# A bidirectional hybrid encoder layer: in its scan one VectorE addition becomes an accumulating DMA, and two VectorE copies move to ScalarE

## The chip, the cores and the metric

The kernel runs on one core of a Trainium2 chip. The metric is device time in microseconds (us) for one execution. A core has TensorE (PE, matrix products; its weight loads are shown as PEld), VectorE (DVE), ScalarE (ACT), GpSimd (POOL) and SyncE (SP), each with an instruction queue of its own that runs in order and waits on semaphores, and 16 engines for DMA transfers, which SP and POOL issue here. SBUF is the on-chip memory with 128 partitions, PSUM the memory that TensorE writes to.

## The reference

One encoder layer over 1024 positions of width 1024: a normalised input is projected to many columns; a convolution branch and a bidirectional gated linear recurrence ("the scan") run side by side; their gated sum is projected and added to the input; a gated feed-forward block with a short convolution follows, and a last norm. The change lies in the scan. Its forward direction is, per head (8 heads of 128 columns):

```python
def _chunk_gated_scan(q, k, v, lf):
    # S_t = diag(f_t) S_{t-1} + k_t v_t^T,  o_t = S_t^T q_t,  lf = log f
    ...
    def step(state, inp):
        qb, kb, vb, lfb = inp
        a = jnp.cumsum(lfb, axis=2)
        diff = a[:, :, :, None, :] - a[:, :, None, :, :]
        decay = jnp.where(tril, jnp.exp(jnp.minimum(diff, 0.0)), 0.0)
        scores = jnp.einsum("bhtk,bhsk,bhtsk->bhts", qb, kb, decay)
        o = (jnp.einsum("bhts,bhsv->bhtv", scores, vb)
             + jnp.einsum("bhtk,bhkv->bhtv", qb * jnp.exp(a), state))
        ...
```

The backward direction is the same on flipped inputs with its own gates, and the two outputs are added: `return o_fwd + o_bwd`. A position therefore meets itself twice, once in each direction. All of it is float32.

## The kernel before

**Stages.** Input norm and the first projections; a convolution of 31 taps on VectorE beside most of the input projections; then, from 540 us to some 990 us, the scan, beside the projections that are left (the generator `dense`); then the output projections, the feed-forward block and the last norm. A float32 product is made of three products of rounded parts (`mm3`, L143 to L145), whose parts ScalarE (L121) and VectorE (L118) prepare.

**Order of the work.** Only TensorE's order is the order in which the program is written (`manual_schedule(engines={PE})`); for the other engines a scheduler plans the order when the program is built, from modelled durations and dependencies, and sets the semaphores.

**The scan.** A head's 1024 positions are taken in two halves of 512, so there are 16 halves, i = 0 to 15, two per head; "even" and "odd" below are by i. In a half, positions lie along the columns, in four chunks of 128. For each half:

- `scan_inputs` (L741) loads q and the gates' inputs and makes the gates `f` and keys `k` with ScalarE (L752, L753, L755) and one VectorE clamp (L762). It is called one half further ahead.
- `scan_base` (L765) works on blocks of eight positions. In the tile DE, made once and used by all halves, it builds running products of gates for both directions: E in its first half, D in its second, eight columns per block, so that the r-th of each block is reached with a stride of eight. L780 copies two such columns, L781 to L798 fill the others with products and a reciprocal (L786). From these it makes Qh (L730 by way of L809) and Kh (L733), then qF and kG. All but the gates is VectorE's. It runs one half ahead, two steps at a time.
- `scan_levels` (L825) makes the 128 x 128 score blocks S_t of the four chunks. Positions that share a block of eight come from `inside(d)`, one product per direction, laid into S_t under the masks m_f and m_b. The backward product's diagonal can't be laid over the forward one, so it is collected under the mask m_d in the tile dg (L867), of which only the diagonal is ever not zero. Then come the levels 8, 16, 32 and 64: at level h each pair of neighbouring blocks of h positions is joined, by a copy A of kG's halves (ScalarE, L835), four matmuls into a PSUM bank (L838), an update of kG, the move of the level's part of the product into S_t, an update of qF (both updates are L730), and a product of the small tile tb. The next level's matmuls need the updated qF. The part that belongs to a level is that in which row and column differ by an exclusive-or from h to 2h - 1: levels 16 and 32 are laid in by VectorE under the masks m_16 and m_32 (L869, all 128 x 512 elements read), level 64 by ScalarE as two blocks of 64 partitions (L873), level 8 is a whole copy by ScalarE (L862) that comes first. Last, L885 adds dg to S_t on VectorE.
- `scan_states` (L887) turns kG over (transposes L894, copies kT L896), forms the chunk's contribution to the states (L903) and carries the states on (L911, L921).
- `outputs` (L985) of a head are made in the steps of the next head's even half: the backward states (L989), then for each half the products with S_t, v and the states (L942), a copy (L944), four Squares with sums (L948), the reciprocal root on POOL (`rstd_small`, L404 and L405), the scaling (L955), a transpose (L963) and VectorE's product `ev` (L965).

**What lies between.** After each step of `scan_levels` and `scan_states`, `between` lets the dense projections advance, then the next half's base, then the outputs of the head before:

```python
            def between(fill):
                dense.fill(fill)
                if ahead is not None:
                    ahead.step(BASE_STEPS)
                pending.fill(1)
```

S_t has three buffers, dg and DE one, qF three. POOL has no DMA to issue during the scan; in the projections before and in the feed-forward block after it, `pair_job` issues accumulating DMAs there (L238).

Of the kernel before, what the change touches and what calls it, by code (L numbers as in the profile page):

```python
# [13 lines left out]
U8 = mybir.dt.uint8  # L14
AF = mybir.ActivationFunctionType
ALU = mybir.AluOpType
AX = mybir.AxisListType

P = 128
# [15 lines left out]
def view(t, off, dims):  # L35

    return bass.AP(
        tensor=t.tensor,
        offset=t.offset + off,
        ap=[list(t.ap[0])] + [list(d) for d in dims],  # L40
    )
# [3 lines left out]
def tile_hybrid_encoder(  # L45
# [24 lines left out]
    V, A, G, T = nc.vector, nc.scalar, nc.gpsimd, nc.tensor  # L70

    S, D = x.shape[1], x.shape[2]
# [10 lines left out]
    cp = ctx.enter_context(tc.tile_pool(name="const", bufs=1))  # L83
# [7 lines left out]
    def nm(s):  # L91
        uid[0] += 1
        return f"{s}_{uid[0]}"
# [3 lines left out]
    def bank(tag):  # L97
        return ps.tile([P, H], F32, tag=tag, name=nm(tag), bufs=BANKS[tag])
# [13 lines left out]
    def load(src):  # L112
        t = tmp()
        nc.sync.dma_start(t, src)
        return t
# [438 lines left out]
    m_b = cp.tile([P, P], U8, name="m_b")  # L554
    m_d = cp.tile([P, P], U8, name="m_d")
    m_16 = cp.tile([P, P], U8, name="m_16")
    m_32 = cp.tile([P, P], U8, name="m_32")

    def build_masks():
        it = mp.tile([P, P], I32, tag="tm", name=nm("it"), bufs=4)  # L560
        ip = mp.tile([P, P], I32, tag="tm", name=nm("ip"), bufs=4)
        G.iota(it, pattern=[[1, P]], base=0, channel_multiplier=0)
        G.iota(ip, pattern=[[0, P]], base=0, channel_multiplier=1)
        xo = mp.tile([P, P], I32, tag="tm", name=nm("xo"), bufs=4)
        V.tensor_tensor(xo, it, ip, op=ALU.bitwise_xor)
        fs = mp.tile([P, 4, P], F32, tag="tm", name=nm("fs"), bufs=4)
        V.tensor_copy(fs[:, 0, :], xo)
        V.tensor_tensor(fs[:, 1, :], it, ip, op=ALU.subtract)
        ge = fs[:, 1, :]
        V.tensor_scalar(m_d, fs[:, 0, :], 0.0, None, op0=ALU.is_equal)  # L570
        V.tensor_scalar(fs[:, 2, :], fs[:, 0, :], 8.0, None, op0=ALU.is_lt)
        V.tensor_scalar(fs[:, 3, :], ge, 0.0, None, op0=ALU.is_ge)
        V.tensor_tensor(m_f, fs[:, 2, :], fs[:, 3, :], op=ALU.mult)
        V.tensor_scalar(fs[:, 3, :], ge, 0.0, None, op0=ALU.is_lt)
        V.tensor_tensor(m_b, fs[:, 2, :], fs[:, 3, :], op=ALU.mult)
        for m, h in ((m_16, 16.0), (m_32, 32.0)):
            V.tensor_scalar(fs[:, 2, :], fs[:, 0, :], h, None, op0=ALU.is_ge)
            V.tensor_scalar(fs[:, 3, :], fs[:, 0, :], 2 * h, None, op0=ALU.is_lt)
            V.tensor_tensor(m, fs[:, 2, :], fs[:, 3, :], op=ALU.mult)

    build_masks()

# [129 lines left out]
    for k in range(NK2):  # L712
        t = load(d_h[k][1])
# [7 lines left out]
    dg = hp.tile([P, H], F32, name="dg")  # L721
# [7 lines left out]
    def tt(o, a, b, op=ALU.mult):  # L729
        V.tensor_tensor(o, a, b, op=op)  # L730

    def keys(o, a, scale, b):
        V.scalar_tensor_tensor(o, a, scale, b, op0=ALU.mult, op1=ALU.mult)  # L733
# [4 lines left out]
    def c4(t):  # L738
        return t.rearrange("p (c t) -> p c t", c=4)
# [25 lines left out]
    def scan_base(ins):  # L765


        q, f, kk, ks = ins

        def two(t, *r):  # L770
            if len(r) == 1:
                return view(t, r[0], [[8, N2]])
            return view(t, r[0], [[r[1] - r[0], 2], [8, N2]])

        fv = lambda *r: two(f, *r)
        ed = lambda *r: two(DE, *r)
        D = D0


        V.tensor_copy(ed(2, D + 4), fv(3, 4))  # L780
        tt(ed(1, D + 5), fv(2, 4), fv(3, 5))  # L781
        yield
        tt(ed(0, D + 6), fv(1, 6), ed(1, D + 5))
        tt(ed(D + 7), ed(D + 6), fv(7))
        yield
        V.reciprocal(ed(D, 7), ed(0, D + 7))  # L786
        yield

        fm = hp.tile([P, 2, NB], F32, tag="fm", name=nm("fm"), bufs=2)
        turned = view(fm, NB, [[-NB, 2], [1, NB]])  # L790
        tt(turned, view(f, 0, [[H, 2], [8, NB]]), view(DE, E0, [[H, 2], [8, NB]]))
        tb = hp.tile([P, 3, NB], F32, tag="tb", name=nm("tb"), bufs=3)
        tt(tb[:, 0:2, :], turned, view(DE, D + 7, [[H, 2], [8, NB]]))
        V.tensor_copy(tb[:, 2, :], tb[:, 0, :])
        tt(ed(D + 1, 6), ed(D, 7), fv(1, 7))
        yield
        tt(ed(D + 2, 5), ed(D + 1, 6), fv(2, 6))
        tt(ed(4), ed(5), fv(5))  # L798
        yield

        qF = hp.tile([P, 2, H], F32, tag="qF", name=nm("qF"), bufs=3)
        kG = hp.tile([P, 2, H], F32, tag="kG", name=nm("kG"), bufs=2)
        Qh = hp.tile([P, 2, H], F32, tag="Qh", name=nm("Qh"), bufs=1)
        Kh = hp.tile([P, 2, H], F32, tag="Kh", name=nm("Kh"), bufs=1)
        along = [[8, NB], [1, 8]]
        for d in range(2):
            m0, st = ((0, 1), (7, -1))[d]
            whole = [[8, NB], [st, 8]]
            tt(view(Qh, (1 - d) * H + m0, whole), view(q, m0, whole), view(DE, D + d * H, along))  # L809
            yield  # L810
            keys(
                view(Kh, d * H + m0, whole),
                view(kk, d * H + m0, whole),
                ks[:, d : d + 1],
                view(DE, d * H, along),
            )
            yield
        both = [[H, 2], [8, NB], [1, 8]]
        tt(view(qF, 0, both), view(Qh, 0, both), view(fm, 0, [[NB, 2], [1, NB], [0, 8]]))
        yield  # L820
        tt(view(kG, 0, both), view(Kh, 0, both), view(DE, D + 7, [[H, 2], [8, NB], [0, 8]]))
        yield
        yield qF, kG, [(Qh[:, 1 - d, :], Kh[:, d, :]) for d in range(2)], tb

    def scan_levels(base, S_t, Tt):  # L825


        qF, kG, qk, tb = base

        def pairs(t, h):  # L830
            return view(t, 0, [[2 * h, H // (2 * h)], [H + h, 2], [1, h]])

        def level(h):
            A_t = page(hp, "A", 2)
            A.copy(A_t.rearrange("p (b x e) -> p b x e", x=2, e=h), pairs(kG, h))  # L835
            b = bank("sc")
            for c in range(4):
                T.matmul(  # L838
                    b[:, c * P : (c + 1) * P].rearrange("p (b x e) -> p b x e", x=2, e=h),
                    A_t[:, c * P : (c + 1) * P],  # L840
                    view(qF, c * P, [[2 * h, P // (2 * h)], [H + h, 2], [1, h]]),
                    start=True,
                    stop=True,
                )
            return c4(b)

        def inside(d):
            b = bank("ob" if d else "sc")
            for c in range(4):
                sl = slice(c * P, (c + 1) * P)  # L850
                T.matmul(b[:, sl], qk[d][1][:, sl], qk[d][0][:, sl], start=True, stop=True)
            return c4(b)

        def over(m):
            return view(m, 0, [[0, 4], [1, P]])

        for h in (8, 16, 32, 64):
            n, nb = H // (2 * h), H // h
            b = level(h)
            tt(pairs(kG, h), pairs(kG, h), view(tb, 1, [[2, n], [nb - 1, 2], [0, h]]))  # L860
            if h == 8:
                A.copy(S_t, b)  # L862
                for d, m in ((0, m_f), (1, m_b)):
                    bi = inside(d)
                    V.copy_predicated(S_t, over(m), bi)
                    if d == 1:
                        V.copy_predicated(c4(dg), over(m_d), bi)  # L867
            elif h < 64:
                V.copy_predicated(S_t, over(m_16 if h == 16 else m_32), b)  # L869
            else:  # L870
                for s0 in range(0, P, h):
                    t0 = s0 ^ h
                    A.copy(S_t[s0 : s0 + h, :, t0 : t0 + h], b[s0 : s0 + h, :, t0 : t0 + h])  # L873
            tt(pairs(qF, h), pairs(qF, h), view(tb, nb + 1, [[2, n], [nb - 1, 2], [0, h]]))
            if h < 64:
                tn = hp.tile([P, 3, NB], F32, tag="tb", name=nm("tb"), bufs=3)
                k = 3
                to = view(tn, 0, [[n, 3], [1, n]])
            else:
                k = 2  # L880
                to = view(Tt, 0, [[4, 2], [1, n]])
            tt(to, view(tb, 0, [[nb, k], [2, n]]), view(tb, 1, [[nb, k], [2, n]]))
            tb = tn
            yield
        V.tensor_tensor(S_t, S_t, c4(dg), op=ALU.add)  # L885

    def scan_states(i, kG, v, Tt, Sf, Sb):  # L887

# [122 lines left out]
    for h in range(NH):  # L1011
# [4 lines left out]
        for half in range(2):  # L1016
# [11 lines left out]
            S_t = hp.tile([P, 4, P], F32, tag="S", name=nm("S"), bufs=3)  # L1028
            vl = load(d_v[h][half])
            for n, _ in enumerate(scan_levels(base, S_t, Tt[:, half])):  # L1030
                if n == 2:
                    b = bank("tr")
# [339 lines left out]
```

## Time and profile before

The median of three runs is 1899.92 us (1898.41 to 1903.82). One execution was profiled:

| profiled execution | us | share of the span |
|---|---|---|
| its time | 1905.6 | |
| span, first to last instruction | 1903.8 | |
| TensorE busy | 1799.7 | 95% |
| VectorE busy | 1270.2 | 67% |
| ScalarE busy | 799.2 | 42% |
| GpSimd busy | 210.9 | 11% |
| granted TensorE clock, mean | 0.977 | |

The views used below: the page's line of busy times; the table of stretches, whose rows give the stretch, its length and then the busy time and the count of instructions of TensorE, its weight loads, VectorE, ScalarE and GpSimd, then the granted clock, the share of the DMA engines and GB/s; the waits, whose rows name who waited, for whom, the total in us, how often and the longest; the timeline, every instruction with start and duration; and the chain of waits, which is followed back from the last instruction to whatever released each step. Names such as `sc<-qF,A` are output and inputs, buffer numbers left out; where a helper records an operation, the line is the helper's (L730 for every `tt`).

### The profile page before, as it was taken

The page shows a single profiled execution, that of the slowest core. Times are in us where ns is not written, and L with a number is a line of the kernel's source. Part 1 is how long each engine was busy: PE and PEld are TensorE (multiplying, and loading weights), DVE is VectorE, ACT ScalarE, POOL GpSimd, SP SyncE. Part 2 cuts the span into 40 slices and gives each one's busy share as a digit, 9 for nine tenths or more (in the row PEclk, how much of TensorE's full clock was granted, in tenths as well). Part 3 has the DMA queues.
Part 4 walks back from the last instruction along what each step waited for, and adds up shares of the span by engine and source line. Part 5 has one row for each costly group of instructions (what it writes and reads, how often), then busy time and mean ns, then how long its engine had stood idle before and what let it go on. Part 6 is the DMA issues. An engine that isn't in the chain of part 4 may idle for free.

```text
span 1903.8 us, 23750 instructions
## 1 busy us (share of the span) xinstructions
PE 1799.7 (95%) x8543; PEld 1484.0 (78%) x8543; DVE 1270.2 (67%) x1860; ACT 799.2 (42%) x1488; POOL 210.9 (11%) x218
## 2 busy tenths in 40 slices
PE   6988999999999998999998999899999999999996
PEld 5767878887778887888786888588888888788885
DVE  3488999535469898999835555667676666534445
ACT  6433333234554554555443134544343344522124
POOL 3101111213100001000100000111111111000000
PEclk9999999999999999999998999899999999999998
DMA  7747788786563333342237665777676676733134
GB/s 256 219 119 169 179 188 199 185 182 148 190 192 89 113 108 96 111 122 82 75 95 216 197 200 183 185 153 154 147 151 143 143 156 128 221 93 96 54 89 162
DMA packets 323916, 285.09 MB, mean 150 GB/s; under 512 B 14926, under 2 KB 245078, under 8 KB 323798
## 3 DMA queue, kind: packets, MB, share of 16 engines
q1 hardware_dynamic: 272006, 242.67, 41.5%
q0 software_dynamic: 51792, 40.90, 15.2%
q8 instruction: 67, 1.10, 0.3%
q14 instruction: 51, 0.42, 0.1%
HBM read 191.24 MB, written 71.83 MB: 138 GB/s over the span
## 4 chain that ended last, share of the span: by engine, by line
PE 66%; DVE 13%; DMA 8%; ACT 6%; issue 3%; POOL 2%; SPq 0%; ACTq 0%; POOLq 0%; DVEq 0%
PE mm L143 16%; PE mm L144 16%; PE mm L145 16%; PE sc L144 3%; PE sc L145 3%; PE sc L143 3%; PE tr L143 2%; PE tr L144 2%; PE tr L145 2%; DVE wp L118 1%; DVE kG L730 1%; DVE DE L730 1%; PE sc L838 1%; DVE qF L730 1%; DMA wr<-wr 1%
## 5 line engine op out<-in xcount | busy, mean ns | idle before, releaser
L143 PE MATMUL mm<-hx,wp 128*128 128x512 f32 x1176 | 482.6, 410 | 24.6 <-ACT hx L121 8.6
L145 PE MATMUL mm<-hx,wp 128*128 128x512 f32 x1176 | 467.4, 397 | 3.9 <-DVE wp L118 3.9
L144 PE MATMUL mm<-hx,wp 128*128 128x512 f32 x1176 | 466.8, 397 | 2.9 <-POOL hx L118 1.9
L121 ACT CAST wp<-wr 128x1024 fp32r<-128x1024 f32 (+2 forms) x196 | 179.7, 917 | 323.0 <-PE mm L144 222.9
L143 PEld LDWEIGHTS mm<-hx,wp 128*128 128x128 f32 x1176 | 226.5, 193 | 73.7 <-ACT hx L121 9.5
L118 DVE TENSOR_TENSOR wp<-wr,wp 128x1024 fp32r<-128x1024 f32 (+2 forms) x196 | 206.9, 1056 | 102.9 <-ACT wp L121 97.4
L145 PEld LDWEIGHTS mm<-hx,wp 128*128 128x128 f32 x1176 | 225.5, 192 | 55.1 <-DVE wp L118 5.4
L144 PEld LDWEIGHTS mm<-hx,wp 128*128 128x128 f32 x1176 | 226.5, 193 | 48.4 <-POOL hx L118 3.6
L645 DVE SCALAR_TENSOR_TENSOR acc<-gl,v_b,acc 128x1024 f32<-128x1024 f32 x120 | 150.1, 1285 | 0.5
L143 PE MATMUL sc<-hy,wq 128*128 128x512 f32 x244 | 97.3, 399 | 3.1 <-ACT hy L121 3.0
L144 PE MATMUL sc<-hy,wq 128*128 128x512 f32 x244 | 96.7, 396 | 2.7 <-DVE hy L118 2.7
L145 PE MATMUL sc<-hy,wq 128*128 128x512 f32 x244 | 96.2, 394 | 0.0
L238 POOL DMA_DIRECT2D wr<-sw x39 | 34.9, 896 | 519.3 <-DVE wp L118 297.4
L1251 DVE TENSOR_TENSOR xr<-mm,xr 128x512 f32<-128x512 f32 x48 | 33.1, 690 | 82.0 <-PE mm L145 82.0
L838 PEld LDWEIGHTS sc<-qF,A 128*128 128x128 f32 x512 | 65.9, 193 | 19.0 <-issue 13.3
L838 PE MATMUL sc<-qF,A 128*128 128x128 f32 x512 | 69.1, 278 | 11.7 <-DVE qF L730 10.6
L121 ACT CAST wq<-sw 128x1024 fp32r<-128x1024 f32 x39 | 41.1, 1054 | 86.6 <-PE mm L144 66.4
L143 PE MATMUL mm<-hy,wp 128*128 128x512 f32 x156 | 63.2, 405 | 7.4 <-ACT wp L121 5.3
L266 ACT COPY su<-mm 128x512 f32<-128x512 f32 x78 | 45.5, 583 | 53.4 <-PE mm L145 53.4
L835 ACT COPY A<-kG 128x512 f32<-128x512 f32 x64 | 39.7, 620 | 66.3 <-DVE kG L730 37.8
L1169 DVE SCALAR_TENSOR_TENSOR tm<-gp,v_a,tm 128x512 f32<-128x512 f32 x88 | 65.6, 746 | 1.8 <-ACT tm L1165 0.9
L1153 DVE TENSOR_TENSOR ft<-su,mm 128x512 f32<-128x512 f32 x22 | 15.1, 687 | 71.6 <-issue 68.1
(281 smaller groups left out, 3548.6 us busy)
## 6 DMA issues: line engine op xcount, KB each, us to landing
wr<-in_w_in_dram SPq DMA_DIRECT2D x55, 512.0 KB, 6.5
sw<-in_ffn_w_up_dram SPq DMA_DIRECT2D x44, 256.0 KB, 3.5
sw<-in_ffn_w_up_dram POOLq DMA_DIRECT2D x22, 512.0 KB, 8.3
wr<-in_ffn_w_up_dram SPq DMA_DIRECT2D x22, 512.0 KB
d_g<-ft SPq DMA_DIRECT2D x44, 256.0 KB, 5.9
ev<-d_g SPq DMA_DIRECT2D x44, 256.0 KB, 3.2
wr<-sw POOLq DMA_DIRECT2D x39, 256.0 KB, 3.3
wr<-wr POOLq DMA_DIRECT2D x39, 256.0 KB, 3.8
```

The source lines that it names most:

```text
L118: eng.tensor_tensor(lo, src, hi.bitcast(F32), op=ALU.subtract)
L121: A.copy(hi, src)
L143: T.matmul(acc, whi[:, k, :], ahi, start=first, stop=False, skip_group_check=again)
L144: T.matmul(acc, whi[:, k, :], alo, start=False, stop=False, skip_group_check=again)
L145: T.matmul(acc, wlo[:, k, :], ahi, start=False, stop=last, skip_group_check=again)
L238: G.dma_start(o, a, accum_op=ALU.add)
L266: A.copy(t, acc)
L645: V.scalar_tensor_tensor(acc, g[:, k : k + S], tap(k), acc, op0=ALU.mult, op1=ALU.add)
L730: V.tensor_tensor(o, a, b, op=op)
L835: A.copy(A_t.rearrange("p (b x e) -> p b x e", x=2, e=h), pairs(kG, h))
L838: T.matmul(b[:, c * P : (c + 1) * P].rearrange("p (b x e) -> p b x e", x=2, e=h), A_t[:, c * P : (c + 1) * P], view(qF, c * P, [[2 * h, P ...
L1169: V.scalar_tensor_tensor(c, g[:, o + k : o + k + H], vec("fdw", k * NF + j), c, op0=ALU.mult, op1=ALU.add,)
```

## The change

Three edits in the scan, and one tile less:

- The strided copy L780 of a half's base is issued on ScalarE rather than on VectorE.
- Level 32 is no longer laid into S_t under a mask. The branch that copies blocks with ScalarE now serves both 32 and 64; for 32 it makes four copies of 32 partitions by 4 x 32 columns. The mask m_32 is not built.
- dg is added to S_t by a DMA that POOL issues and that accumulates into its destination, 128 rows of 2 KB, in place of VectorE's addition.

```diff
@@ masks
-    m_32 = cp.tile([P, P], U8, name="m_32")
...
-        for m, h in ((m_16, 16.0), (m_32, 32.0)):
-            V.tensor_scalar(fs[:, 2, :], fs[:, 0, :], h, None, op0=ALU.is_ge)
-            V.tensor_scalar(fs[:, 3, :], fs[:, 0, :], 2 * h, None, op0=ALU.is_lt)
-            V.tensor_tensor(m, fs[:, 2, :], fs[:, 3, :], op=ALU.mult)
+        V.tensor_scalar(fs[:, 2, :], fs[:, 0, :], 16.0, None, op0=ALU.is_ge)
+        V.tensor_scalar(fs[:, 3, :], fs[:, 0, :], 32.0, None, op0=ALU.is_lt)
+        V.tensor_tensor(m_16, fs[:, 2, :], fs[:, 3, :], op=ALU.mult)
@@ scan_base
-        V.tensor_copy(ed(2, D + 4), fv(3, 4))
+        A.copy(ed(2, D + 4), fv(3, 4))
         tt(ed(1, D + 5), fv(2, 4), fv(3, 5))
@@ scan_levels
-            elif h < 64:
-                V.copy_predicated(S_t, over(m_16 if h == 16 else m_32), b)
+            elif h == 16:
+                V.copy_predicated(S_t, over(m_16), b)
             else:
                 for s0 in range(0, P, h):
                     t0 = s0 ^ h
...
-        V.tensor_tensor(S_t, S_t, c4(dg), op=ALU.add)
+        G.dma_start(S_t.rearrange("p c t -> p (c t)"), dg, accum_op=ALU.add)
```

## The prediction

> **What bounds the kernel now.** I read the page's line of busy times first, then the table of stretches, and found the stage that the change touches: the scan, from 540 us to some 990 us.
>
> ```profile
> PE 1799.7 (95%) x8543; PEld 1484.0 (78%) x8543; DVE 1270.2 (67%) x1860; ACT 799.2 (42%) x1488; POOL 210.9 (11%) x218
> 780.00:840.00 60.00, 57.19 (x381) 51.12 (x380) 57.19 (x106) 35.24 (x87) 3.60 (x6) 1.00 0.35 106
> ```
>
> Over the run VectorE (DVE) is busy 67%, but in this minute of the scan 57.19 of 60 us, exactly as much as TensorE (PE); ScalarE (ACT) has 35.24, GpSimd (POOL) 3.60. So VectorE is full there, yet TensorE is too, and only TensorE's idle time can be won. The view of waits, for TensorE and the scan alone, says how much that is:
>
> ```profile
> PE sc L838 <- DVE qF L730: 10.6, 9, 2.8
> PE tr L894 <- ACT kT L896: 7.4, 3, 2.9
> PE tr L894 <- DVE ev L965: 3.9, 3, 1.7
> PE tr L963 <- ACT tm L955: 3.3, 2, 2.0
> ```
>
> With the small ones it is 30.4 us: 16.4 end with VectorE (10.6 + 3.9 + 1.4 + 0.5) and 14.0 with ScalarE. The timeline shows where they fall. In odd halves TensorE waits for the update of qF: seven times that of level 16, twice (705.1 and 967.2 us) that of level 32. In even halves, which also carry the output work of the head before, it waits after level 64 for kT, `tm` or `ev`. Last I read the chain of waits, which tells whether an instruction that leaves VectorE was on the path at all. A piece of it (start, us, what):
>
> ```profile
> 784.15 0.64 DVE S L869
> 784.79 0.57 DVE qF L730
> ...
> 788.46 0.35 DVE DE L780
> ...
> 792.73 0.63 DVE S L885
> 793.36 0.67 DVE ev L965
> 794.02 0.04 issue
> 794.07 0.66 PE tr L894 x4
> ```
>
> All three removed instructions stand here, one behind the other, ahead of a transpose that waits 1.70 us for `ev`.
>
> **What is removed.** Per half, one L869 (level 32), one L885 and one L780 leave VectorE. Their durations are 0.73, 0.68 and 0.42 us, but VectorE starts the next instruction before one has ended: from start to start the timeline shows 0.62, 0.60 and 0.32 us. That is 1.54 x 16 = 24.6 us of VectorE. It isn't 24.6 us of time: in most halves VectorE idles somewhere (41.6 of 420 us from 540 to 960) and the relief ends there. The chain holds five of the sixteen L869 of level 32 (0.65, 0.65, 0.63, 0.64, 0.73: 3.3 us), four L885 (2.4) and five L780 (1.7): 7.4 us, the most that one can gain in an unchanged order. Each piece shortens only the next wait of TensorE, so I go through these: before 571.7 us 0.34; before 595.7 two pieces, limited to the wait of 0.80; before 633.3 (2.91) three pieces, 1.59; before 685.7 0.65; at 705.1 0.63; before 734.8 (1.39) 0.93; at 794.1 1.62 of 1.70, of which I take 0.8, since kT's copy on ScalarE (794.56) comes next; at 967.2 0.73. Sum **-6.5 us**.
>
> The three instructions of the mask m_32 (0.2 to 0.3 us each, about 151 to 156 us) are costed at nothing: there the chain runs through loads and TensorE; without that cover they would be 0.8 us.
>
> **What ScalarE takes on.** Four blocks of 32 x 128 from PSUM: no such row exists. The nearest are L923, 128 x 128 from PSUM at 0.27 us, and L873, 64 x 256 at 0.36; I take 0.27 by the equal free size, 1.1 us per half (1.5 by the upper row). The strided copy of 128 x 256: between L923 (0.27) and L835, 128 x 512 strided at 0.62; I take 0.40, near the line through L923 and L921 (128 x 384, 0.48). Together 1.5 us x 16 = 24 us, and ScalarE goes from 35 to some 39 of 60 us.
>
> Where it lies decides. The blocks must wait for the four matmuls of level 32, and what is queued behind them on ScalarE waits too. It isn't the copy A of level 64: at 777.43 it already runs, right after level 16's matmuls. In odd halves ScalarE then has idle stretches of 1 to 4 us, so the blocks cost nothing. In even halves the Squares L948 of the output work follow, and behind them GpSimd's rstd (L404, L405), for which ScalarE then idles 1.40 us (783.94 to 785.34). The blocks fit into that hole if they come behind the fourth Square: cost 0. If they come ahead, the rstd, L955 and kT are late by 1.1 us in each of seven even halves: 7.7 us. I take 0, since these Squares are issued ahead of the blocks in program order. The strided copy may start when the base's last Kh has read DE (786.0 us in that half), and ScalarE is back to back from 786.5 to 792.5. Its own consumer, the product Qh, comes some 10 us later, so it is hidden itself; but kT's copy may be pushed by 0.40. I charge the three waits for kT: 3 x 0.4 = **+1.2 us** (from 0 to 7 x 0.62 = 4.3).
>
> **The accumulating DMA.** Sixteen issues on POOL. Nearest rows: L238's adds of the same 256 KB, issue 0.88 (wr<-sw) and landing after 3.3 us, or 3.8 for wr<-wr. It waits for the second L873 and for dg, so it can start at 790.6 us, be issued by 791.5 and land by 795.4. Who needs it: L942 of the outputs, at the tightest 13.5 us after L885 (969.15 to 982.70), and the next L867, which overwrites dg, 10.9 us after it at the tightest (792.73 to 803.63, so still 8 us spare). Cost 0 behind that cover; even the slowest landing of L238, 10.8 us, would end before that L867. Were the cover gone, 16 x 3.8 us of waiting would stand on the path. Queued behind it on POOL is only L404 of the outputs, 1.3 us after that L873: an issue of 0.9 leaves 0.4 spare. Queue time of 16 x 256 KB on transfer engines that are 35% busy: nothing.
>
> **Sum.** -6.5 + 1.2 = -5.3 us. The profiled execution took 1905.6 us, 1903.8 of span and 1.8 around it; it becomes 1900.3. The median of the runs is 5.7 below the profiled one, 1899.92, so I forecast **1894.6 us**.
>
> **Rivals.**
>
> *ScalarE becomes the pacer (slower).* If blocks and copy both come ahead of the Squares and kT in the seven even halves, 7 x 1.5 = 10.4 us are added, and of the relief only the pieces before qF and Sf waits are left: 0.34 + 0.80 + 0.63 + 0.73 = 2.5. Net +7.9, 1908 us. For it: 7.4 + 3.3 us of TensorE's waits already end with ScalarE, and seven pairs of L873 lie on the chain. Against it: the hole of 1.40 us. It decides as soon as more than about 0.9 us per even half is not absorbed.
>
> *GpSimd is held while it issues.* In this stage POOL's rstd is stretched: L404 takes 0.19 us as a rule and once 2.81, L405 1.01 and once 4.01. If the issue is stretched by 3 us as L405 was, it takes 3.9 instead of 0.9, less the 1.3 us spare: L404, L955 and kT are 2.6 us late. In all seven even halves that is 18, less 6.5: +12; at the rate of the trace (3 of 16 of the L405/L404 pairs clearly stretched) only 1 to 2 such cases, which with the relief give -1. Chance for the bad form 0.05, 1906 to 1912 us. [...]
>
> *VectorE waits for ScalarE's copy.* L781 writes other columns of the same tile DE right behind L780. If the two are ordered as writes to one tile, VectorE waits for ScalarE's queue, 1 to 3 us per half: 16 to 48 us, net at least +10. No two engines write interleaved columns in the trace before, so nothing there excludes it; chance 0.05.
>
> *The new plan is better.* Only TensorE's order is written out; the other engines are planned anew. If L869 and L885 being gone lets every qF update move up 0.6 us, the five later waits of level 16 (648.7 to 909.6 us, 5.1 us together) vanish too: -6.5 - 5.1 = -11.6, 1888 us.
>
> *Nothing passes through.* Waits move from VectorE to ScalarE in equal size: -1, 1899 us.
>
> **How the numbers follow.** Forecast 0.48 (its own range -2 to -10, 1890 to 1898); better plan 0.13; ScalarE the pacer 0.18; GpSimd held 0.05; wait on DE 0.05; nothing 0.11. A measurement of this kernel tells some 0.3% (5.7 us) from no change. The forecast's case lies a little over half beyond that (0.27), the rest within (0.21). Faster 0.27 + 0.13 = 0.40; same 0.21 + 0.11 = 0.32; slower 0.28. The range takes in the better plan to -15 and the pacer to +10: 1885 to 1910; left out are most of the wait on DE and the ends of the better plan and of GpSimd held.
>
> **What would show it.** VectorE busy in 540 to 960 down from 378 to some 354 us; waits of L838 for qF at 10.6 down to 7 or 8, and those at 705 and 967 gone or halved; L942 and L867 never waiting for a DMA. ScalarE's copies: blocks near 0.27, the strided one near 0.40. Wrong it is if waits for kT and `tm` (7.4 and 3.3) grow by more than 5 us together, if L404 starts later behind its Squares, if a VectorE wait for a ScalarE write to DE appears, or if waits for qF stay as they are.

## The result, and the profile after

The changed kernel takes 1917.13 us (median of 6 runs, 1914.45 to 1920.72), the kernel before in the same comparison 1901.87 (1898.34 to 1911.81). The ratio is 1.0085, with a 95% interval from 1.0064 to 1.0105: slower by 0.85%, outside the forecast range and on its other side. The profiled execution took 1920.6 us with a span of 1918.8, so 15.0 more span than before. Nearly all of it arises in the scan: its last product with S_t (L942 before, L940 after; every line from L780 on has moved up by two) starts at 984.81 us before and at 998.73 after, 13.9 us later.

The page's line of busy times of the kernel after (busy us, share of the span, instructions):

```profile
PE 1804.1 (94%) x8543; PEld 1483.5 (77%) x8543; DVE 1242.7 (65%) x1809; ACT 822.6 (43%) x1568; POOL 236.6 (12%) x234
```

And two rows of its table of stretches:

```profile
780.00:840.00 60.00, 53.38 (x334) 46.72 (x332) 47.29 (x88) 34.56 (x89) 8.84 (x6) 0.97 0.38 108
540.00:960.00 420.00, 385.11 (x2373) 333.20 (x2371) 344.32 (x634) 243.56 (x567) 48.53 (x40) 0.99 0.37 107
```

VectorE did get its relief: from 540 to 960 us it is busy 344.32 us, against 378.41 before. TensorE nevertheless does less in the same time (385.11 against 392.34). In the stretch from 780 to 840 us, which was full before, VectorE now has 12.7 us idle and TensorE 6.6. The number to stop at is GpSimd's: 8.84 us for six instructions, two of them DMA issues of 0.92 and 0.93; before, its six instructions took 3.60.

The waits of TensorE in the scan (who waited, for whom; total us, times, longest):

```profile
PE tr L961 <- ACT kT L894: 9.7, 3, 4.6
PE sc L836 <- DVE qF L728: 8.6, 10, 1.8
PE tr L892 <- DVE ev L963: 5.8, 2, 3.3
PE tr L961 <- ACT tm L953: 4.3, 5, 1.7
```

All of TensorE's waits there come to 39.9 us, against 30.4. Those for qF, most of them in the odd halves, fell a little, as foreseen. The others grew, and not in one place: kT from 7.4 to 9.7 with single waits of 4.6 us, `ev` from 3.9 to 5.8, `tm` from 3.3 to 4.3, and the states Sf and Sb from 2.6 to 7.6 us. The waits of ScalarE and of VectorE lead one step further back. ScalarE after:

```profile
ACT tm L953 <- POOL ors L405: 33.2, 16, 5.2
```

and the same row of the kernel before:

```profile
ACT tm L955 <- POOL ors L405: 26.7, 16, 4.0
```

VectorE after:

```profile
DVE f L760 <- ACT f L753: 39.2, 9, 8.5
```

ScalarE waits 33.2 us for the reciprocal root on GpSimd against 26.7, and VectorE, relieved of work, waits 39.2 us for the gates that ScalarE makes (13.9 before). The timeline shows one such place. First the kernel before, in an even half (start us, us, engine, line, operation, output and inputs; in brackets the idle time before it and who ended it):

```profile
783.47 0.68 DVE L730 TENSOR_TENSOR Qh<-q,DE 128x512 f32<-128x512 f32 x1
...
784.02 0.19 POOL L404 TENSOR_SCALAR ors<-oss 128x4 f32<-128x4 f32 x1 [41.51 <-ACT jk L948]
...
784.07 0.71 DVE L869 COPY_PREDICATED S<-m,sc 128x512 f32<-128x512 uint8 x1
...
784.30 1.01 POOL L405 TENSOR_TENSOR ors<-ors,mhalf 128x4 f32<-128x4 f32 x1
...
784.68 0.67 DVE L730 TENSOR_TENSOR qF<-qF,tb 128x512 f32<-128x512 f32 x1
...
785.34 0.40 ACT L955 ACTIVATE tm<-tm,ors 128x128 f32<-128x128 f32 x1 [1.40 <-POOL ors L405]
```

And the same place in the kernel after:

```profile
782.87 0.71 DVE L728 TENSOR_TENSOR Qh<-q,DE 128x512 f32<-128x512 f32 x1
...
782.98 0.65 POOL L404 TENSOR_SCALAR ors<-oss 128x4 f32<-128x4 f32 x1 [20.61 <-ACT jk L946]
...
783.47 0.77 DVE L731 SCALAR_TENSOR_TENSOR Kh<-k,kscale,DE 128x512 f32<-128x512 f32 x1
...
783.72 5.05 POOL L405 TENSOR_TENSOR ors<-ors,mhalf 128x4 f32<-128x4 f32 x1
...
784.13 1.24 DVE L728 TENSOR_TENSOR qF<-Qh,fm 128x1024 f32<-128x1024 f32 x1
...
785.27 1.24 DVE L728 TENSOR_TENSOR kG<-Kh,DE 128x1024 f32<-128x1024 f32 x1
...
787.16 0.70 DVE L728 TENSOR_TENSOR qF<-qF,tb 128x512 f32<-128x512 f32 x1
...
787.90 0.21 DVE L728 TENSOR_TENSOR tb<-tb 128x48 f32<-128x48 f32 x1
...
788.80 0.40 ACT L953 ACTIVATE tm<-tm,ors 128x128 f32<-128x128 f32 x1 [5.02 <-POOL ors L405]
...
798.11 0.58 ACT L894 COPY kT<-tr 128x512 f32<-128x512 f32 x1
```

Before, L405, the second instruction of the root, starts while VectorE lays in level 32, and takes 1.01 us. After, that masked copy is gone. Product follows product on VectorE from 782.87 to 788.11 us, each with two inputs in SBUF, and L405 takes 5.05 us: it ends at 788.77, 0.66 after the last of them. ScalarE stands idle for 5.02 us in front of the scaling, and what it runs after that is late, down to kT's copy at 798.11, which starts 7.22 us after the transposes that it reads have ended (3.59 in the kernel before) and for which TensorE waits 4.64 us. The same happens twice more: L405 at 841.02 takes 5.06 us and VectorE's run ends 0.65 before it does; at 898.04 it takes 4.40, and 0.89 before its end the products break off for 0.28 us, in which VectorE waits for TensorE.

The kernel before has one L405 of this kind, and it shows how narrow the opening is. Its timeline near 937 us:

```profile
936.99 0.73 DVE L869 COPY_PREDICATED S<-m,sc 128x512 f32<-128x512 uint8 x1
...
937.59 4.01 POOL L405 TENSOR_TENSOR ors<-ors,mhalf 128x4 f32<-128x4 f32 x1
...
937.61 0.67 DVE L730 TENSOR_TENSOR qF<-qF,tb 128x512 f32<-128x512 f32 x1
...
938.21 1.22 DVE L730 TENSOR_TENSOR kG<-Kh,DE 128x1024 f32<-128x1024 f32 x1
...
939.34 1.22 DVE L118 TENSOR_TENSOR wp<-wr,wp 128x1024 fp32r<-128x1024 f32 x1
```

There L405 starts at 937.59, 0.13 us before the masked copy ends (at 784.30 it was 0.48 before), and takes 4.01 us: it ends at 941.60, 0.87 after the last of the products behind the copy.

### The profile page after: what moved, and what is told of

Same layout as the page of the kernel before. It is cut to its first block, busy times and chain, and to the rows that moved or that the text cites. A ratio compares the mean times of both kernels' runs of the same rounds, so it can differ in the third digit from the quotient of the medians.

```text
span 1918.8 us, 23841 instructions
## 1 busy us (share of the span) xinstructions
PE 1804.1 (94%) x8543; PEld 1483.5 (77%) x8543; DVE 1242.7 (65%) x1809; ACT 822.6 (43%) x1568; POOL 236.6 (12%) x234
## 3 DMA queue, kind: packets, MB, share of 16 engines
q1 hardware_dynamic: 272006, 242.67, 40.9%
## 5 line engine op out<-in xcount | busy, mean ns | idle before, releaser
L121 ACT CAST wp<-wr 128x1024 fp32r<-128x1024 f32 (+2 forms) x196 | 179.7, 917 | 349.1 <-PE mm L144 212.8
L143 PE MATMUL mm<-hy,wp 128*128 128x512 f32 x156 | 63.5, 407 | 7.2 <-ACT wp L121 5.1
L145 PE MATMUL mm<-hy,wp 128*128 128x512 f32 x156 | 63.0, 404 | 0.0
```

The source lines that it names most:

```text
L121: A.copy(hi, src)
L143: T.matmul(acc, whi[:, k, :], ahi, start=first, stop=False, skip_group_check=again)
L145: T.matmul(acc, wlo[:, k, :], ahi, start=False, stop=last, skip_group_check=again)
```

## The experiments

**The theory** after this reading: the masked copy of level 32 was not only work on VectorE. It broke up VectorE's run of products and was a stretch in which GpSimd's root could get in. Without it the root is held by a longer run, and ScalarE stands behind the root. **Rivals:** ScalarE has become the bound by the blocks and the strided copy it took on; or the DMA holds GpSimd or comes late; or the new plan is worse by itself.

To put a number on the root in every kernel, two sums are taken from each trace: the *delay*, from the end of a half's last Square to the first scaling, summed over the fourteen halves of output work of heads 0 to 6; and the length of the seven even halves in which that work runs (from the copy L862 of the level 8 in halves 2 to 14 to that of the next half), beside the length of the others (halves 0, 1, 3 and so on to 13). Both sums come from one profiled execution of each kernel; how far they vary is seen at the last experiment. Ratios are to the kernel before as run beside each (medians of 1893.88 to 1901.87 us), with 95% intervals.

| kernel | median us | ratio | delay | even halves | others |
|---|---|---|---|---|---|
| before | | 1 | 29.6 | 209.9 | 182.2 |
| after | 1917.13 | 1.0085 [1.0064, 1.0105] | 40.6 | 222.9 | 184.4 |
| after, root left out | 1887.23 | 0.9929 [0.9903, 0.9955] | 13.1 | 194.5 | 185.6 |
| before, root left out | 1882.27 | 0.9920 [0.9894, 0.9946] | 16.7 | 196.7 | 179.7 |
| after, masked copy on VectorE added | 1903.21 | 1.0026 [1.0008, 1.0044] | 26.8 | 205.1 | 189.3 |
| after, level 32 undone | 1914.40 | 1.0075 [1.0040, 1.0111] | 35.5 | 216.9 | 183.6 |
| level 32 alone | 1921.66 | 1.0101 [1.0072, 1.0131] | 44.8 | 231.0 | 180.1 |
| strided copy alone | 1902.02 | 1.0001 [0.9978, 1.0025] | 38.5 | 212.0 | 186.6 |
| DMA alone | 1900.07 | 0.9995 [0.9977, 1.0014] | 33.3 | 213.1 | 181.3 |
| level 32 alone, root left out | 1882.62 | 0.9929 [0.9903, 0.9955] | 16.7 | 199.7 | 178.5 |
| before, root on VectorE | 1919.23 | 1.0101 [1.0079, 1.0123] | 102.8 | 233.3 | 179.6 |
| before, root twice | 1940.01 | 1.0214 [1.0189, 1.0240] | 70.5 | 252.6 | 180.9 |
| before, scaling one step later | 1901.04 | 1.0002 [0.9985, 1.0019] | 34.0 | 216.0 | 179.8 |
| after, scaling one step later | 1920.78 | 1.0113 [1.0091, 1.0135] | 45.1 | 234.3 | 180.6 |

**The root taken out, after and before.** If the loss comes through the root, it must vanish with it.

```diff
-            rstd_small(rs, ss, DK)
+            V.tensor_scalar(rs, ss, 1.0 / DK, EPS, op0=ALU.mult, op1=ALU.add)
```

> The changed kernel, with the scan's scale rs = 1/sqrt(mean square + eps) cut down to mean square + eps and computed by VectorE: the reciprocal root is left out, and GpSimd has no arithmetic in the scan. Theory G (GpSimd's small root waits while VectorE runs instructions with two SBUF inputs, and everything behind it on ScalarE and TensorE waits with it): the even halves fall from 29 to 34 us to 26 to 28 us, the whole to about 1885 to 1895 us, not above the same cut of the kernel before. Rival S (ScalarE's added copies are what is late): the even halves keep most of their length, the whole stays above the same cut of the kernel before by 10 us or more.

> The kernel before with the same cut (the reciprocal root of the scan's output norm is left out, the rest of it on VectorE). Theory G: 7 to 12 us faster than the kernel before, since its own stretched roots (9.9 us over the plain 2.4 per head) go too: 1890 to 1895 us. Rival S: little changes, 1898 to 1902 us.

Measured: ratios 0.9929 and 0.9920, whose intervals overlap almost wholly. The loss of 0.85% is gone as far as these runs can tell (the medians still differ by 5.0 us, within what the intervals allow), and the root turns out to cost the kernel before 0.8% as well, 15.6 us by the medians where 7 to 12 were expected. These two kernels also answer the question of what the three edits are worth without the root: VectorE's relief less ScalarE's added load. TensorE's waits for qF after the change:

```profile
PE sc L836 <- DVE qF L728: 11.6, 10, 2.6
```

and before it:

```profile
PE sc L838 <- DVE qF L730: 10.2, 9, 2.8
```

VectorE is busy 362.30 us of the 420 in the one and 386.50 in the other. The 24.2 us that it has less to do buy TensorE nothing on balance; VectorE's waits for ScalarE grow from 36.7 to 63.0 us (540 to 1000 us) instead; 8.7 us of this growth lie in front of the small instruction that stands in the root's place.

**The window put back.** The kernel after, with a masked copy of the size of the removed one put where the removed one stood, into a tile that nobody reads.

```diff
+    junk_t = hp.tile([P, 4, P], F32, name="junk_t")
...
+    G.memset(junk_t, 0.0)
...
+                if h == 32:
+                    V.copy_predicated(junk_t, over(m_16), b)
```

> The changed kernel, with one masked copy of the level-32 product by VectorE added back at its old place, into a scratch tile that nobody reads. ScalarE keeps its blocks, VectorE gets its 0.73 us per half back. Theory G with a window (the removed masked copy read PSUM and left GpSimd a gap in which the root ran): the stretched roots of 4 to 5 us go back to at most one, the time falls to 1900 to 1908 us although work is added. Rival S, or the DMA: no gain, 1917 to 1925 us.

Measured: 1.0026, so VectorE was given sixteen instructions more, of some 0.7 us, and the kernel became faster, by 0.6 of the 0.85 points (1.0085 to 1.0026). TensorE's waits in the scan go from 39.9 back to 29.7 us. Its timeline at the place that was stretched at 841 us:

```profile
836.06 0.80 POOL L404 TENSOR_SCALAR ors<-oss 128x4 f32<-128x4 f32 x1 [22.60 <-ACT jk L950]
...
836.74 0.72 DVE L875 COPY_PREDICATED junk_t<-m,sc 128x512 f32<-128x512 uint8 x1
...
836.95 1.03 POOL L405 TENSOR_TENSOR ors<-ors,mhalf 128x4 f32<-128x4 f32 x1
...
837.35 1.21 DVE L730 TENSOR_TENSOR qF<-Qh,fm 128x1024 f32<-128x1024 f32 x1
...
838.02 1.28 ACT L957 ACTIVATE tm<-tm,ors 128x128 f32<-128x128 f32 x4 [1.16 <-POOL ors L405]
```

L405 starts inside the useless copy and takes 1.03 us. ScalarE still makes all the blocks and strided copies here, so ScalarE as the bound can't be the main cause. What is left, 0.26%, is not accounted for.

**Level 32 undone**, in the kernel after, with the DMA and the strided copy kept; the mask m_32 is built again (not shown).

```diff
-            elif h == 16:
-                V.copy_predicated(S_t, over(m_16), b)
+            elif h < 64:
+                V.copy_predicated(S_t, over(m_16 if h == 16 else m_32), b)
```

> The change without its level-32 part: masked copy on VectorE again, the DMA and the strided copy as changed. Theory G with the window: most of the loss goes, 1898 to 1906 us. Rival S: ScalarE sheds 16 of its 28 added us, so about half of the loss goes, 1906 to 1912 us. If the DMA or the strided copy is at fault: 1912 to 1920 us.

Measured: 1.0075, a miss. Its timeline says why the masked copy alone didn't help:

```profile
837.28 0.74 DVE L869 COPY_PREDICATED S<-m,sc 128x512 f32<-128x512 uint8 x1
...
837.92 0.67 DVE L730 TENSOR_TENSOR qF<-qF,tb 128x512 f32<-128x512 f32 x1
...
838.28 0.97 POOL L404 TENSOR_SCALAR ors<-oss 128x4 f32<-128x4 f32 x1 [22.52 <-ACT jk L948]
...
839.33 5.08 POOL L405 TENSOR_TENSOR ors<-ors,mhalf 128x4 f32<-128x4 f32 x1
```

The copy is there, but the last Square ends at 838.18, after it, and the root arrives when the products have begun: 5.08 us. How sharply this divides is seen when all root instructions that start while a masked copy runs are gathered, at level 32 or at any other, from the traces of before, after and the eight kernels of this section that keep the root on GpSimd:

| masked copy still to run when L404 or L405 starts | instructions | their durations |
|---|---|---|
| 0.20 to 0.68 us | 31 | L404 0.19, L405 1.01 to 1.04 |
| 0.05 to 0.16 us | 5 | L404 3.22, 5.96, 6.49; L405 3.98, 4.01 |

Not one is in between. Of these 36, none that started well inside a masked copy was held, and each that started in its last 0.16 us was, beside the products that follow. So it hangs on tenths of a microsecond of ScalarE's plan whether the copy helps.

The same ten traces say more about what lets the root in. Two other VectorE operations are of one kind (SCALAR_TENSOR_TENSOR, 128 x 512), but `ev` takes its data from PSUM and Kh reads two tiles in SBUF. Of the root's instructions that start beside `ev`, none of 32 is held (0.19 or 0.20 and 1.01 to 1.04 us); of those that start beside Kh, all 33 are (in the kernels before and after these are six L405 of 1.42 to 5.06 us). So it is not the kind of the operation. Nor is it simply the number of tiles read in SBUF: beside the reciprocal, which reads one, none of 12 is held (0.19 and 1.01 us before), but beside the clamp of `f`, which reads one too, all 9 are (L405 1.33 before, L404 0.39 after).

**Each edit alone.** The kernel before with one of the three edits.

```diff
@@ level 32 alone
-            elif h < 64:
-                V.copy_predicated(S_t, over(m_16 if h == 16 else m_32), b)
+            elif h == 16:
+                V.copy_predicated(S_t, over(m_16), b)
@@ strided copy alone
-        V.tensor_copy(ed(2, D + 4), fv(3, 4))
+        A.copy(ed(2, D + 4), fv(3, 4))
@@ DMA alone
-        V.tensor_tensor(S_t, S_t, c4(dg), op=ALU.add)
+        G.dma_start(S_t.rearrange("p c t -> p (c t)"), dg, accum_op=ALU.add)
```

> Of the three edits only the level-32 one: four ScalarE blocks, no masked copy on VectorE; VectorE keeps the strided copy and the addition of dg. Theory G (GpSimd's root gets in only where VectorE runs something other than two-SBUF-input work): the masked copy was the gap in which the root ran in five of seven heads, so roots of over 2 us appear in three heads or more, and the time is 8 to 16 us above the kernel before. If the masked copy is not what matters, within 4 us of the kernel before.

> Of the three edits only the strided copy on ScalarE (0.71 us there against 0.42 on VectorE). Theory G: ScalarE's Squares end later and VectorE's run of two-input work loses the copy that stood in it, so roots are stretched if they come behind the masked copy: 0 to 10 us above the kernel before. Rival S (ScalarE's load by itself): 11 us of ScalarE in the scan, 3 to 6 us above the kernel before with no stretched root.

> Of the three edits only the accumulating DMA in place of the addition of dg. Nobody waited for it in the changed kernel (landing 3.3 to 5.1 us, needed after 10 or more), so I expect the kernel before within 4 us; were the DMA's issue on GpSimd at fault, 8 us or more above it.

Measured: 1.0101, 1.0001 and 0.9995. Level 32 alone makes the whole loss, 20 us by the medians and so more than the 8 to 16 expected; each of the other two alone costs nothing and brings nothing. The timeline of level 32 alone shows the held root again, now in its first instruction:

```profile
782.43 0.26 ACT L871 COPY S<-sc 32x128 f32<-32x128 f32 x1
...
782.49 4.06 POOL L404 TENSOR_SCALAR ors<-oss 128x4 f32<-128x4 f32 x1 [42.40 <-ACT jk L946]
...
782.98 1.21 DVE L728 TENSOR_TENSOR qF<-Qh,fm 128x1024 f32<-128x1024 f32 x1
```

There is no DMA on GpSimd in this kernel's scan, so the DMA's issue doesn't hold it.

**Level 32 alone, root left out.** The blocks stay on ScalarE, the root goes.

> The level-32 edit alone with the root cut as in the two cut runs (the reciprocal root of the scan's output norm is left out, mean square plus eps on VectorE). Theory G: the edit's own loss, 1.0% with the root on GpSimd, vanishes: a ratio of 0.990 to 0.994 to the kernel before, as the cut kernel before (0.992). Rival S: the four blocks on ScalarE cost by themselves and the ratio stays at 0.998 or above. If VectorE's relief of 10 us is worth something: 0.987 or below.

Measured: 0.9929, against 0.9920 for the kernel before with the same cut. With the root, level 32 costs 1.0%; without it, nothing that can be told from nothing. The blocks on ScalarE cost no more than the relief of VectorE gives; the two are not told apart here.

**The root on VectorE.** Were GpSimd's wait the trouble, another engine might make the root: twelve dependent instructions on 128 x 4 values in place of L404 and L405.

```diff
+    def rstd_vector(dst, ss, n):
+        V.tensor_scalar(x, ss, 1.0 / n, EPS, op0=ALU.mult, op1=ALU.add)
...
+        for k in range(3):
+            V.tensor_tensor(t, y, y, op=ALU.mult)
+            V.scalar_tensor_tensor(t, t, -0.5, x, op0=ALU.mult, op1=ALU.mult)
+            V.scalar_tensor_tensor(dst if k == 2 else y, t, 1.5, y, op0=ALU.add, op1=ALU.mult)
...
-            rstd_small(rs, ss, DK)
+            rstd_vector(rs, ss, DK)
```

> The kernel before with the whole reciprocal root of the scan's output norm on VectorE: a first guess by integer arithmetic on the bits and three Newton steps, twelve instructions on 128 x 4 elements, about 1.5 us of VectorE per half. Theory G: GpSimd's wait is gone as in the cut version (1882 us against 1898), less what 24 us more on a full VectorE costs: 1884 to 1893 us. If a full VectorE is the bound, it is no faster than before.

Measured: 1.0101, a miss. The twelve stand one by one between the scan's products in VectorE's queue, so the delay is 102.8 us, far longer than with GpSimd. Who pays is plain in TensorE's waits in this kernel:

```profile
PE tr L975 <- ACT tm L967: 26.1, 8, 5.0
```

**The root twice**, the first into a spare tile, on GpSimd.

```diff
+            extra = cp.tile([P, 4], F32, name=nm("extra"), tag="extra", bufs=2)
+            rstd_small(extra, ss, DK)
             rstd_small(rs, ss, DK)
```

> The kernel before with GpSimd's root computed twice, first into a spare tile: some 1.2 us more between the last Square and the scaling, sixteen times, nothing else changed. If delay there is paid for nearly in full in the even halves: 14 x 1.2 = 17 us at most, I expect 8 to 18 us above the kernel before. If TensorE has slack for it: within 3 us.

Measured: 38 us slower, where 8 to 18 were expected. The delay grows by 40.9 us and the even halves by 42.7. From before to after it was 11.0 and 13.0, from before to before without the root -12.9 and -13.2: in these three steps a microsecond of delay costs 1.0 to 1.2 us of the even halves, so little hides the root. What I had underrated is the delay itself, put at 17 us at most: two more instructions on GpSimd are two more that can be held, and here four L405 take 4.7 to 5.9 us and one L404 4.0. The price isn't a law for every kernel: level 32 alone gives 1.4 (15.2 of delay, 21.1 of halves), the root on VectorE 0.3 (73.2 and 23.4), the strided copy alone 0.2 (8.9 and 2.1).

**The scaling one step later**, before and after: a `yield` moved so that L955 is written behind the next step's work.

```diff
+            yield
...
-            yield
```

> The kernel before, with one step moved: the four scalings L955 of a half's outputs are issued after the next step rather than right behind the root, so that ScalarE need not stand and wait for GpSimd. Theory G, and that the wait for the root is what costs: the even halves fall from 210 to about 197 us in sum, as without GpSimd's arithmetic, 1882 to 1892 us, though roots may still be stretched in the trace. If the root's delay only goes with the loss and doesn't cause it: 1896 to 1902 us.

> The changed kernel with the same step moved. Theory G: the loss of 16 us goes and what the plain kernel before still pays goes too, 1883 to 1893 us, within 6 us of the kernel before with the step moved. Rival S (ScalarE's load): it stays 8 us or more above that one. If VectorE's relief is worth what I forecast once the root is out of the way, it is 3 to 7 us below that one.

Measured: 1.0002 and 1.0113. Neither tests anything, since ScalarE's planned order came out the same: the scaling still stands right behind the root, and ScalarE waits for it 31.1 us in the one and 36.3 in the other. In fact the order of the instructions is that of the kernel before, or after, on every engine, so the two rows are in effect repeats of the first two. As such they are worth having. The loss is there again (1.0113), and the two sums show how far one trace is to be trusted: the delay differs from the first trace by 4.4 and 4.5 us and the even halves by 6.1 and 11.4, while the step from before to after is 11.1 and 18.3 where it was 11.0 and 13.0. Smaller differences in the table say nothing.

## Why the prediction was wrong

**The step that failed** is the one under "What is removed": the masked copy of level 32 was priced as relief alone, its part of the -6.5 us, and the only loss considered for its going was that of the blocks on ScalarE ("The blocks fit into that hole ... cost 0"). That hole of 1.40 us was the root itself, at its undisturbed 1.01 us. I took the root's duration as fixed, though in the traces it differs with what VectorE runs at that moment (L405 1.01 us at 784.30 before, 5.05 at 783.72 after), and the change takes away an instruction beside which it could run. In place of -6.5 + 1.2 the runs show two terms: the relief less ScalarE's load is worth nothing that can be seen (0.9929 against 0.9920 with the root gone from both), and the held root, with +11.0 us of delay, goes with even halves that are longer by 13.0 of the span's 15.0 us.

**The rival "GpSimd is held while it issues"** had the right victim, the right path (L404 and L405, the scaling, kT) and, at its worst of +12, nearly the right size, but the wrong cause, and so a chance of 0.05. The size is luck: it was 18 us of delay less 6.5 of relief, where the runs show 11.0 of delay and no relief. The issue is not stretched (0.85 to 0.93 us; the 39 issues of wr<-sw before took 0.88 to 0.95), and the loss is there without any DMA (1.0101 with level 32 alone). What the traces show is a root that is long beside VectorE's products: L405 takes 4.40 to 5.06 us beside a run of products with both inputs in SBUF, and 1.01 to 1.04 when it starts well inside a masked copy, whose data come from PSUM. By what means it is held is not shown. The rows that should have led to this reading were in the trace of before: L405 at 937.59 with 4.01 us, started in the last 0.13 us of an L869, against 784.30 with 1.01, started in the middle of one. I had read them as a rate of accidents, not asked what ran beside them.

**The rival "ScalarE becomes the pacer"** gave 1908 us for another reason. The blocks do come ahead of the fourth Square, against what I took (L871 at 782.43 above, its last one, is issued behind the Squares, but three others stand between them), because ScalarE's order is planned and does not follow the program's text; with the root left out this costs nothing beyond what the relief gives.

**"Nothing passes through"** (waits move from VectorE to ScalarE) describes the relief well: VectorE's waits for ScalarE in the scan (540 to 1000 us) grow from 43.3 to 72.4 us.

The sign named for a failure, waits for kT and `tm` growing by more than 5 us together, didn't show: they grew by 3.3 (2.3 and 1.0), the rest spread over states and `ev`. Of the other signs, a wait for the copy in DE did appear, but once and of 0.3 us, and L404 starts 0.1 us behind its last Square as before, but once 0.44. What showed it was the row of ScalarE's waits for GpSimd, which the prediction did not name.

**Right:** VectorE's busy time fell (378.41 to 344.32, further than the 354 foreseen, the scan being slower as well); the waits for qF fell from 10.6 to 8.6 and the two of level 32 (at 705 and 967 us) are gone, though with the root left out they rose instead (10.2 to 11.6), so this fall can't be put down to the relief; nobody waited for the accumulating DMA, whose landing took 3.3 to 5.1 us and issue 0.85 to 0.93; the blocks took 0.24 to 0.26 us (0.27 assumed). **Mis-sized, without effect that the runs show:** the strided copy on ScalarE takes 0.71 us, not 0.40. **Misread:** the longest of the nine waits for qF before, 2.8 us at 571.7, lies in half 0, an even half, not an odd one.

**Open.** The edits are not additive: strided copy and DMA cost nothing alone and 0.75% together, where the root again came too late for the copy; that the plan of ScalarE decides this is read from one timeline and not tried. Which property of the masked copy lets the root in was not tried either; the rows beside `ev` and Kh point to its data in PSUM. Nor is it known why a root that has started well inside it then runs on beside the next product, or why some runs of products let one in after 1.3 to 2.0 us (L405 at 885.54 and 623.39 before) and others only after 4 to 5. TensorE's waits account for 9.5 of the 15.0 us. No version that beats both kernels and makes the root was found; the kernels without it run 0.7 to 0.8% faster than the kernel before.

## What to carry to other kernels

Before an instruction is taken off a full engine, look at what other engines run beside it: it may be a time in which a small instruction elsewhere gets through, as L405 did here in 1.01 us beside the masked copy. A small operation whose duration varies in the trace (L405 1.01 or 4.01 us, L404 0.19 or 2.81, each time on 128 x 4 values) is a question to answer before predicting, by reading what stands beside the short and the long ones. And a small step in a chain that goes from GpSimd over ScalarE to TensorE is priced by its latency, not by its busy share: here a microsecond of delay mostly cost one or more, though as little as 0.2 in one kernel.

## What the runs showed of the hardware

- The same GpSimd instruction on 128 x 4 values took 1.00 to 1.04 us or up to 5.94 (L405), 0.19 or up to 6.49 (L404), by what VectorE ran beside it; started 0.20 us or more before the end of a masked copy from PSUM it was never held (31 of 31), 0.16 or less before it always (5 of 5).
- Started beside one and the same VectorE operation it was held in all 33 cases when both tiles lie in SBUF (Kh; L405 1.42 to 5.06 us before and after), and in none of 32 when the data come from PSUM (`ev`; 0.19 or 0.20 and 1.01 to 1.04 us).
- The issue of an accumulating DMA by GpSimd in the same stage is not stretched: 0.85 to 0.93 us, sixteen times.
- On ScalarE a copy of 128 x 256 with a stride of eight in both input and output takes 0.67 to 0.76 us, longer than its strided 128 x 512 copy A (0.62).
